# A two-layer decoder step on one Trainium2 core: where the feed-forward network applies the row scale, and how four small states are laid out and stored

## The chip, the cores and the metric

The program runs on one core of one Trainium2 chip. The core has a matrix engine, TensorE (PE in the profile; PEld is its weight load), and four others: VectorE (DVE), ScalarE (ACT), GpSimd (POOL) and SyncE (SP). Each takes its own instructions in order, and they meet through semaphores. Matrix products are accumulated in PSUM, in banks of 128 x 512 float32; everything else lies in SBUF, in 128 partitions. DMAs move data between the device memory and SBUF. In this program nearly all of them are issued by SP, one after the other; a few are issued by ACT.

The metric is the device time of one execution in microseconds (us); lower is better. Several executions are timed, and the median counts.

## The reference

One step of a hybrid decoder with 2 layers, for a prompt of 256 positions and 8 samples of one position each, so for T = 264 columns. Width is 1024, the inner width of the feed-forward network (FFN) is 2816. Each layer is a mixer with an input and an output projection, and then this FFN:

```python
def conv_ffn(x, prev, norm_g, w_gate, w_up, conv_w, conv_b, w_down):
    T = x.shape[1]
    h = rmsnorm(x, norm_g)
    g = h @ w_gate
    g_all = jnp.concatenate([prev, g], axis=1)
    gc = sum(conv_w[i] * g_all[:, i:i + T] for i in range(CONV_W)) + conv_b
    a = jax.nn.gelu(gc) * (h @ w_up)
    return x + a @ w_down, g_all[:, -(CONV_W - 1):]
```

`rmsnorm(x, g)` is `x * rsqrt(mean(x*x) + eps) * g`: a factor R for each position, and a gain for each feature. Since R belongs to the position, `(x * g) @ w * R` gives the same product as `rmsnorm(x, g) @ w`.

Layer 1 also has a pooling mixer (running means over windows of 2, 4, 8 and 16 positions). Outputs beside y are the keys and values of both layers, and states: the last 15 pooling inputs (`pool_prompt`, `pool_sample`) and the last 2 gate rows of the FFN (`ffn_conv_prompt`, `ffn_conv_sample`).

## The kernel before, in words

**Layout.** Activations are transposed: features on the 128 partitions, the 264 positions along the row. Every weight matrix is cut into blocks of 128 x 128, and the host packs all 1,472 blocks in the order in which PE uses them. To come near float32 accuracy, each operand is split into a high and a low part (`wh`, `wl` for weights, `..._h`, `..._l` for activations), and a block is three matmuls of 264 columns: high x high, high x low, low x high (`run`, L306).

**Weights.** SP loads chunks of 16 blocks (1 MB, tile `raw`, three buffers). `split` (L292) makes tiles of 8 blocks out of them: ACT copies the high part (L300) and DVE subtracts it for the low part (L301). There are four buffers of `wh` and of `wl`, and `split` runs three tiles ahead of PE.

**Phases.** For each layer: `in` (input projection, with attention and the other mixer woven in by hooks), `out` (output projection), `ff` (gate and up projection) and `dn` (down projection). In `ff` the order is gate 0, up 0, gate 1, up 1 and so on for 22 pairs; an output tile takes 8 blocks, 24 matmuls, and one of four PSUM banks (pool `psm`, `MMB = 4`). For the first four output tiles the blocks are taken in two halves.

**FFN.** `residual` (L589) leaves the operand `xg`: x times the gain, without R. The first `JN = 5` pairs multiply `xg`; R is multiplied in when the product leaves PSUM (L561 for the gate, L575 for up), and for up POOL then multiplies by the activated gate (L576). Meanwhile `normalise` (L549) builds a second operand `xn` that holds R: POOL multiplies x by R (L551), ACT makes the high part (L385) and DVE the low part (L386), for each of 8 tiles. Pairs 5 to 21 multiply `xn`; their gate is read from PSUM by the convolution itself (ACT L564, DVE L565 and L566, ACT L568), and one DVE instruction (L578) multiplies up by the activated gate. `halves` (L432) then splits the result `a` into its parts (ACT L433, DVE L434) for `dn`.

**States.** `CSTATE` holds the 2 old gate rows of the 8 samples for both layers, with the row index inside the feature index; `conv_prep` (L531) weights them on POOL and stores the newer row as `cs0` and `cs1` (L538). `PALL` has 16 places per feature group and sample: places 0 to 14 are loaded (L935), place 15 is written by `pool_in` (L1024), and places 1 to 15 are stored as `pools` (L1088). `plp`, the last 15 pooling inputs of the prompt, is stored as `poolp` (L1087).

**Order.** A scheduler of the framework orders each engine's instructions by its own estimate of time; instructions given to `keep_in_program_order` keep the order in which the code calls them. `late` (L274) is such a DMA on SP. Hooks (`blk(b, f)`) call f when b blocks of the phase have been issued. The stores of `k1`, `v1`, `poolp` and `pools` are plain DMAs: their place in SP's queue is the scheduler's. In the queue that results, `pools` and `poolp` stand behind the second `raw` load of layer 1's input projection and ahead of the loads of the cached values `V` (8 tiles in 16 DMAs).

**Layer 1's input projection.** Among its hooks: `pool_mix` (four products of the pooling mixer), `zs_score` and `zs_tr` (the samples' attention: scores, a scan `keep_s` and weights `zs` on ACT and DVE, and the transposes `pP` on PE), `z_qk` and `z_tr` (the prompt's attention).

Of the kernel before, what the change touches and what calls it, by code (L numbers as in the profile page):

```python
# [9 lines left out]
F32 = mybir.dt.float32  # L10
# [4 lines left out]
ALU = mybir.AluOpType  # L15
# [3 lines left out]
P = 128  # L19
D = 1024  # L20
KD = D // P
SEQ = 256
NS = 8
T = SEQ + NS
# [7 lines left out]
NF = DFF // P  # L32
# [1 line left out]


MMB = 4
JN = 5
KQ = 5
WARM = 12
YD = ((0, 1), (1, 3), (3, 5), (5, 7), (7, 8))  # L40

NA = 4
NB_ = 0.5
NEG = -1e30
SCALE = HD ** -0.5
POOLW = (2, 4, 8, 16)
NST = 15
# [106 lines left out]
def _consts():  # L154
# [35 lines left out]
_INS = [  # L190
    ("w", ((_NB - 16) * P * P,)), ("xw", (P * (KD + 16 * P + KD * T),)), ("x", (P, KD * T)), ("vec", (P, _NVEC)), ("cst", _CST_ARR.shape), ("rope", (P, 2 * T)),
    ("kt0", (NPHYS, P, 512)), ("vp0", (NPHYS, P, 512)), ("kt1", (NPHYS, P, 512)), ("vp1", (NPHYS, P, 512)),
    ("cstate", (P, 2 * NF * 2 * NS)), ("pstate", (P, 4 * NS * NST)),
    ("sguw", (P, 512)), ("sgub", (P, 512)), ("poolw", (P, 512)),
]
_OUTS = [
    ("y", (KD, P, T)), ("k0", (P, 4, T)), ("v0", (P, 4, T)), ("bvn", (P, 4, NS)),
    ("k1", (P, 4, T)), ("v1", (P, 4, T)), ("poolp", (P, 4, NST)), ("pools", (P, 4, NS, NST)),
    ("cv0", (P, NF, 10)), ("cv1", (P, NF, 10)), ("cs0", (P, NF, NS)), ("cs1", (P, NF, NS)),
]  # L200

# [2 lines left out]
def tile_decoder_step(ctx: ExitStack, tc: tile.TileContext, a):  # L204
    nc = tc.nc
    v, s, g = nc.vector, nc.scalar, nc.gpsimd
# [16 lines left out]
    con = ctx.enter_context(tc.tile_pool(name="con", bufs=1))  # L223
# [4 lines left out]
    sm = ctx.enter_context(tc.tile_pool(name="sm", bufs=3))  # L228
# [6 lines left out]
    def mv(name):  # L235
        return [f4(f"{name}_{x}", dt=F32R) for x in "hl"]

    def hl(tiles, k):
        return tiles[k // 4][0][:, k % 4, :], tiles[k // 4][1][:, k % 4, :]
# [4 lines left out]
    X = con.tile([P, KD, T], F32, name="X")  # L244
    VEC = con.tile([P, _NVEC], F32, name="VEC")
    CST = con.tile([P, _CST_ARR.shape[1]], F32, name="CST")
    PT = con.tile([1, NS * NPG], I32, name="PT")
    CSTATE = con.tile([P, 2, NF, 2, NS], F32, name="CSTATE")
    C0 = con.tile([P, 2, NF, NS], F32, name="C0")
    PALL = con.tile([P, 4, NS, 16], F32, name="PALL")  # L250

# [4 lines left out]
    def vec(n):  # L256
        o, w = _VEC[n]
        return VEC[:, o:o + w]
# [15 lines left out]
    def late(dst, src):  # L274
        tc.keep_in_program_order(nc.sync.dma_start(dst, src))
# [59 lines left out]
    orders = dict(_PHASES)  # L335
# [9 lines left out]
    first, o = [], 0  # L345
# [37 lines left out]
    def operand_tile(dst, m, src, gain, pin=False):  # L383
        h, l = dst[0][:, m % 4, :], dst[1][:, m % 4, :]
        i = s.activation(h, src, AF.Copy, scale=gain)  # L385
        j = v.scalar_tensor_tensor(l, src, gain, h.bitcast(F32), ALU.mult, ALU.subtract)  # L386
        if pin:
            tc.keep_in_program_order(i)
            tc.keep_in_program_order(j)
# [141 lines left out]
    def conv_prep(l):  # L531
        cw = vec("cw")
        w = lambda i: cw[:, (l * 3 + i) * NF:(l * 3 + i + 1) * NF].unsqueeze(2).to_broadcast([P, NF, NS])
        t = sm.tile([P, NF, NS], F32, tag="cprep", name=f"cprep{l}", bufs=1)
        g.tensor_tensor(C0[:, l], CSTATE[:, l, :, 0, :], w(0), ALU.mult)
        g.tensor_tensor(t, CSTATE[:, l, :, 1, :], w(1), ALU.mult)
        g.tensor_tensor(C0[:, l], C0[:, l], t, ALU.add)
        nc.sync.dma_start(a[f"cs{l}"], CSTATE[:, l, :, 1, :])  # L538

    def ffn(l, xg, R, down_evac, hooks=None):  # L540
        cw, cb = vec("cw"), vec("cb")
        wc = lambda i, j: cw[:, (l * 3 + i) * NF + j:(l * 3 + i) * NF + j + 1]
        cvo = sm.tile([P, NF, 10], F32, tag="cvo", name=f"cvo{l}", bufs=1)
        act = [mv(f"a{l}_{i}") for i in range((NF + 3) // 4)]
        xn = [mv(f"xn{l}{i}") for i in range(2)]
        gain = vec(f"f{l}")
        half = {}

        def normalise(m):  # L549
            z = sm.tile([P, T], F32, tag="rz", name=f"xr{l}{m}", bufs=4)  # L550
            g.tensor_tensor(z, X[:, m, :], R, ALU.mult)  # L551
            operand_tile(xn[m // 4], m, z, gain[:, m:m + 1])

        def evac(m, o):
            n, j = m
            if n == "g":
                wk = f4(f"wk{l}_{j}", (P, 2, T))
                C = wk[:, 0, :]
                if j < JN:
                    G = wk[:, 1, :]  # L560
                    v.tensor_tensor(G, o, R, ALU.mult)  # L561
                else:
                    G = o
                s.activation(C, G, AF.Identity, scale=wc(2, j), bias=cb[:, l * NF + j:l * NF + j + 1])  # L564
                v.scalar_tensor_tensor(C[:, 1:SEQ], G[:, 0:SEQ - 1], wc(1, j), C[:, 1:SEQ], ALU.mult, ALU.add)  # L565
                v.scalar_tensor_tensor(C[:, 2:SEQ], G[:, 0:SEQ - 2], wc(0, j), C[:, 2:SEQ], ALU.mult, ALU.add)  # L566
                v.tensor_tensor(C[:, SEQ:T], C[:, SEQ:T], C0[:, l, j, :], ALU.add)
                s.activation(cvo[:, j, :], G[:, SEQ - 2:T], AF.Copy)  # L568
                s.activation(C, C, AF.Gelu_apprx_tanh)
                half[j] = wk  # L570
            else:
                wk = half.pop(j)
                C, A = wk[:, 0, :], wk[:, 1, :]
                if j < JN:
                    v.tensor_tensor(A, o, R, ALU.mult)  # L575
                    g.tensor_tensor(A, A, C, ALU.mult)  # L576
                else:
                    v.tensor_tensor(A, o, C, ALU.mult)  # L578
                halves(*hl(act, j), A)

        hk = Hooks()
        for m in range(KD):
            hk.at(NA + NB_ * m, normalise, m)
        run(orders[f"ff{l}"], lambda m, k: hl(xg if m[1] < JN else xn, k), evac, hk)
        nc.sync.dma_start(a[f"cv{l}"], cvo)
        lnexp()
        run(orders[f"dn{l}"], lambda m, k: hl(act, k), down_evac, hooks)
# [22 lines left out]
    xg = [mv(f"xg_0{i}") for i in range(2)]  # L610
# [63 lines left out]
    q4, k4, v4 = f4("q4"), f4("k4"), f4("v4")  # L674
# [185 lines left out]
    hk = Hooks()  # L860
    fixed[0] = True
    blk = lambda b, f, *x: hk.at(b / 8 - 1, f, *x)
# [45 lines left out]
    hk = Hooks()  # L908
# [5 lines left out]
        blk(8, s_av, t)  # L914


    late(CSTATE, a["cstate"].rearrange("p (l j i s) -> p l j i s", l=2, j=NF, i=2))
    for l in range(2):
        conv_prep(l)

# [3 lines left out]
    R = nrm.finish()  # L924
# [7 lines left out]
    ffn(0, xg, R, evac, hk)  # L932


    late(PALL[:, :, :, 0:NST], a["pstate"].rearrange("p (g s i) -> p g s i", g=4, s=NS))  # L935
    xg = xg1
    q4, k4, v4 = f4("q4b"), f4("k4b"), f4("v4b")
    vt = f4("vt1", (P, 2, 512))
# [130 lines left out]
        blk(b, z_qk, t)  # L1069
    for t, b in enumerate((91, 104, 116)):  # L1070
        blk(b, z_tr, t)
    blk(100, lambda: nc.sync.dma_start(a["k1"], k4))
    for i, b in enumerate((62, 66, 70, 76)):
        blk(b, pool_mix, i)
    for t, b in enumerate((110, 118, 126)):
# [1 line left out]
    for i, b in enumerate((100, 108)):  # L1077
        blk(b, sample_av_of(st1, PZ, vtiles, i, "l1"))
    run(orders["in1"], pick(xg), in1_evac, hk)
    nc.sync.dma_start(a["v1"], v4)  # L1080
    hk = Hooks()
    blk(1, zs_out)
    blk(2, z_tr, 3)
    blk(6, lambda: v_pair(vt, v4[:, 3, :], 3, "v1"))
    for t in range(4):
        blk(9, z_av, t)
    nc.sync.dma_start(a["poolp"], plp)  # L1087
    nc.sync.dma_start(a["pools"], PALL[:, :, :, 1:16])  # L1088

    xg, nrm, evac = residual(vec("f1"), "f1")  # L1090
    run(orders["out1"], pick([catA, catB]), evac, hk)
# [12 lines left out]
def _lay(inp):  # L1104
    f = {n: np.asarray(x) for n, x in inp.items()}
    x = np.concatenate([f["x_prompt"].reshape(SEQ, D), f["x_sample"].reshape(NS, D)])
    col = lambda w: w.reshape(-1, P).T
    kt = lambda c: c[:, :, 0].reshape(NPHYS, P, 4, P).transpose(0, 3, 2, 1).reshape(NPHYS, P, 512)
    vecs = {"n1": col(f["l1_norm"]), "f0": col(f["ffn_norm"][0]), "f1": col(f["ffn_norm"][1]),
            "fin": col(f["final_norm"]), "sg": col(f["l0_sgu_gain"]), "ps": col(f["l1_pool_scale"]),  # L1110
            "cw": col(f["ffn_conv_w"].reshape(-1)), "cb": col(f["ffn_conv_b"].reshape(-1)),
            "w00": np.tile(f["l0_sgu_w"][:, 0, 0][None, :], (P, 1)), "b00": np.tile(f["l0_sgu_b"][:, 0][None, :], (P, 1))}
    ws = _pack_weights(f["l0_w_in"], f["l0_w_out"], f["l1_w_in"], f["l1_w_out"], f["ffn_w_gate"], f["ffn_w_up"], f["ffn_w_down"])
    xt = x.T.reshape(KD, P, T).transpose(1, 0, 2)
    return {
        "w": np.concatenate(ws[2:]),
        "xw": _pack_first(col(f["l0_norm"]), xt, ws),
        "x": xt.reshape(P, KD * T),
        "vec": np.concatenate([vecs[n] for n in _VEC], 1),
        "cst": _CST_ARR,  # L1120
        "rope": _ROPE,
        "kt0": kt(f["cache_l0_kv"]), "vp0": f["cache_l0_kv"][:, :, 1].reshape(NPHYS, P, 512),
        "kt1": kt(f["cache_l1_kv"]), "vp1": f["cache_l1_kv"][:, :, 1].reshape(NPHYS, P, 512),
        "pt": f["page_table"].reshape(1, NS * NPG),
        "cstate": f["state_ffn_conv"].reshape(2, NS, 2, NF, P).transpose(4, 0, 3, 2, 1).reshape(P, -1),
        "pstate": f["state_l1_pool"].reshape(NS, NST, 4, P).transpose(3, 2, 0, 1).reshape(P, -1),
        "sguw": f["l0_sgu_w"].transpose(2, 0, 1).reshape(P, 512),
        "sgub": np.tile(f["l0_sgu_b"].reshape(1, 512), (P, 1)),
        "poolw": f["l1_pool_w"].transpose(1, 0, 2).reshape(P, 512),
    }  # L1130
# [39 lines left out]
```

## Time and profile before

| | |
|---|---|
| time, median of 3 executions | 611.6 us (610.9 to 612.25) |
| the profiled execution | 612.44 us |
| its span, first to last instruction | 610.3 us |
| PE busy | 593.2 us, 97% of the span, 4908 matmuls |
| DVE busy | 417.4 us, 68% |
| ACT busy | 343.8 us, 56% |
| POOL busy | 66.7 us, 11% |
| bytes moved by DMA | 122.23 MB |

An execution is profiled by the hardware; 2.1 us of its time lie outside the span. The page lists groups of instructions as `line engine operation out<-in shape xcount | busy us, mean ns of one | idle us before, and what ended it`. The timeline lists `start us, duration us, engine line operation out<-in`, with the idle time of the engine before in brackets and what ended it. The chain of work is followed back from the last instruction, at each step to what released it. A busy matmul is longer than the distance to the next one, because they are pipelined; what counts is the distance from start to start. SPq and DVEq are the queues that issue.

### The profile page before, as it was taken

What the parts mean: (1) busy time and instruction counts of PE and PEld (TensorE: products, weight loads), DVE (VectorE), ACT (ScalarE), POOL (GpSimd) and SP (SyncE); (2) the same over time, 40 slices, a digit from 0 to 9 for tenths busy, and PEclk for the clock granted to TensorE, in tenths of its full rate; (3) what the DMA queues carried; (4) which work ended last, traced back from release to release, by engine and by line L of the source; (5) the groups of instructions that cost most, each with busy time, mean ns of one, the idle gap of its engine ahead of it and who ended that gap; (6) DMA issues with size and microseconds to landing.
All of it is one profiled execution on the core that took longest, in us unless ns stands there. A gap on an engine that the chain in (4) does not pass through costs nothing.

```text
span 610.3 us, 12279 instructions
## 1 busy us (share of the span) xinstructions
PE 593.2 (97%) x4908; PEld 573.3 (94%) x4908; DVE 417.4 (68%) x711; ACT 343.8 (56%) x607; POOL 66.7 (11%) x83
## 2 busy tenths in 40 slices
PE   8999999999999999999999799999999999999994
PEld 7988879999999999999999588999999999999994
DVE  6899566879776766655559276597986766754442
ACT  7757755576655555544454256566665555555441
POOL 4100002341000000011110000033300000001120
PEclk9999999999999999999999999999999999999998
DMA  8998936544654554894579992445365454564502
GB/s 324 347 396 293 333 123 173 200 147 139 213 202 164 182 205 150 333 333 166 201 178 86 262 356 106 169 154 198 133 214 177 169 207 158 189 209 154 199 1 71
DMA packets 41258, 122.23 MB, mean 200 GB/s; under 512 B 17138, under 2 KB 18546, under 8 KB 29810
## 3 DMA queue, kind: packets, MB, share of 16 engines
q1 hardware_dynamic: 40368, 120.25, 60.0%
q10 hardware_dynamic: 834, 1.20, 0.6%
q8 instruction: 38, 0.62, 0.4%
q14 instruction: 18, 0.15, 0.1%
HBM read 117.50 MB, written 3.94 MB: 199 GB/s over the span
## 4 chain that ended last, share of the span: by engine, by line
PE 71%; DVE 3%; DMA 2%; issue 1%; ACT 1%; POOL 0%; DVEq 0%; SPq 0%; ACTq 0%
PE mm L216 68%; DMA raw<-in_w 2%; DVE xn_l L386 1%; DVE wl L301 1%; PE pv_l L216 1%; PE Z L216 1%; PE pav L216 0%; DVE wk L565 0%; PE pt L219 0%; DVE X L1100 0%; DVE wk L566 0%; ACT wh L300 0%; POOL wk L576 0%; DVE wk L561 0%; PE vtp_v L219 0%
## 5 line engine op out<-in xcount | busy, mean ns | idle before, releaser
L301 DVE TENSOR_TENSOR wl<-raw,wh 128x1024 fp32r<-128x1024 f32 x179 | 220.4, 1231 | 132.7 <-ACT wh L300 130.8
L300 ACT ACTIVATE wh<-raw 128x1024 fp32r<-128x1024 f32 x179 | 189.6, 1060 | 184.4 <-PE mm L216 164.0
L216 PE MATMUL mm<-xn_h,wh 128*128 128x264 f32 x544 | 154.7, 284 | 0.0
L216 PE MATMUL mm<-xn_l,wh 128*128 128x264 f32 x544 | 154.5, 284 | 0.0
L216 PE MATMUL mm<-xn_h,wl 128*128 128x264 f32 x544 | 153.4, 282 | 0.0
L216 PEld LDWEIGHTS mm<-xn_h,wh 128*128 128x128 f32 x544 | 102.2, 188 | 0.2 <-ACT cvo L568 0.2
L216 PEld LDWEIGHTS mm<-xn_l,wh 128*128 128x128 f32 x544 | 102.2, 188 | 0.0
L216 PEld LDWEIGHTS mm<-xn_h,wl 128*128 128x128 f32 x544 | 102.2, 188 | 0.0
L216 PE MATMUL mm<-a_l,wh 128*128 128x264 f32 x352 | 99.8, 284 | 0.0
L216 PE MATMUL mm<-a_h,wh 128*128 128x264 f32 x352 | 99.7, 284 | 0.0
L216 PE MATMUL mm<-a_h,wl 128*128 128x264 f32 x352 | 99.3, 282 | 0.0
L216 PEld LDWEIGHTS mm<-a_l,wh 128*128 128x128 f32 x352 | 66.1, 188 | 0.0
L216 PEld LDWEIGHTS mm<-a_h,wl 128*128 128x128 f32 x352 | 66.1, 188 | 0.0
L216 PEld LDWEIGHTS mm<-a_h,wh 128*128 128x128 f32 x352 | 66.0, 188 | 0.0
L216 PE MATMUL mm<-xg_h,wh 128*128 128x264 f32 x160 | 48.2, 301 | 1.3 <-ACT xg_h L385 1.3
L216 PE MATMUL mm<-xg_f_h,wh 128*128 128x264 f32 x160 | 46.0, 288 | 2.0 <-DVE wk L575 2.0
L216 PE MATMUL mm<-xg_l,wh 128*128 128x264 f32 x160 | 46.2, 289 | 0.0
L216 PE MATMUL mm<-xg_h,wl 128*128 128x264 f32 x160 | 46.1, 288 | 0.0
L216 PE MATMUL mm<-xg_f_l,wh 128*128 128x264 f32 x160 | 45.4, 284 | 0.0
L216 PE MATMUL mm<-xg_f_h,wl 128*128 128x264 f32 x160 | 45.1, 282 | 0.0
L216 PE MATMUL mm<-xg_n_h,wh 128*128 128x264 f32 x128 | 39.2, 307 | 0.0
L216 PE MATMUL mm<-xg_n_l,wh 128*128 128x264 f32 x128 | 36.9, 288 | 0.0
(249 smaller groups left out, 1055.5 us busy)
## 6 DMA issues: line engine op xcount, KB each, us to landing
raw<-in_w SPq DMA_DIRECT2D x89, 1024.0 KB, 4.9
K<-in_kt SPq DMA_DIRECT2D x32, 256.0 KB, 6.1
V<-in_vp SPq DMA_DIRECT2D x32, 256.0 KB, 7.2
raw<-in_w SPq DMA_DIRECT2D x4, 512.0 KB, 5.8
X<-in_x SPq DMA_DIRECT2D x4, 264.0 KB
xw<-in_xw SPq DMA_DIRECT2D x2, 388.0 KB, 5.6
out_k<-k SPq DMA_DIRECT2D x1, 528.0 KB
out_v<-v SPq DMA_DIRECT2D x1, 528.0 KB
```

Source lines behind the costliest of these rows:

```text
L216: return self.keep(nc.tensor.matmul(*x, **k))
L300: s.activation(h, src, AF.Copy)
L301: v.tensor_tensor(l, src, h.bitcast(F32), ALU.subtract)
L386: j = v.scalar_tensor_tensor(l, src, gain, h.bitcast(F32), ALU.mult, ALU.subtract)
```

## The change

In the FFN the operand `xn`, `normalise` and its hooks go. All 22 pairs multiply `xg`, and each product is multiplied by R on DVE as it leaves PSUM. The convolution always reads that SBUF copy, and up is always multiplied by the activated gate on POOL. `CSTATE` is laid out with the row index outside, so that a partition's part of `cs0` or `cs1` is one run of 176 floats. `PALL` is loaded and stored whole, 16 places instead of 15 (the host pads the input and drops one place of the output). `poolp`, `pools`, `k1` and `v1` go through `late`, at fixed block numbers.

```diff
-JN = 5
-NA = 4
-NB_ = 0.5
...
-    CSTATE = con.tile([P, 2, NF, 2, NS], F32, name="CSTATE")
+    CSTATE = con.tile([P, 2, 2, NF, NS], F32, name="CSTATE")
...
-        g.tensor_tensor(C0[:, l], CSTATE[:, l, :, 0, :], w(0), ALU.mult)
-        g.tensor_tensor(t, CSTATE[:, l, :, 1, :], w(1), ALU.mult)
+        g.tensor_tensor(C0[:, l], CSTATE[:, l, 0], w(0), ALU.mult)
+        g.tensor_tensor(t, CSTATE[:, l, 1], w(1), ALU.mult)
         g.tensor_tensor(C0[:, l], C0[:, l], t, ALU.add)
-        nc.sync.dma_start(a[f"cs{l}"], CSTATE[:, l, :, 1, :])
+        nc.sync.dma_start(a[f"cs{l}"], CSTATE[:, l, 1])
...
-        xn = [mv(f"xn{l}{i}") for i in range(2)]
-        gain = vec(f"f{l}")
         half = {}
-
-        def normalise(m):
-            z = sm.tile([P, T], F32, tag="rz", name=f"xr{l}{m}", bufs=4)
-            g.tensor_tensor(z, X[:, m, :], R, ALU.mult)
-            operand_tile(xn[m // 4], m, z, gain[:, m:m + 1])
 
         def evac(m, o):
             n, j = m
             if n == "g":
                 wk = f4(f"wk{l}_{j}", (P, 2, T))
                 C = wk[:, 0, :]
-                if j < JN:
-                    G = wk[:, 1, :]
-                    v.tensor_tensor(G, o, R, ALU.mult)
-                else:
-                    G = o
+                G = wk[:, 1, :]
+                v.tensor_tensor(G, o, R, ALU.mult)
...
-                if j < JN:
-                    v.tensor_tensor(A, o, R, ALU.mult)
-                    g.tensor_tensor(A, A, C, ALU.mult)
-                else:
-                    v.tensor_tensor(A, o, C, ALU.mult)
+                v.tensor_tensor(A, o, R, ALU.mult)
+                g.tensor_tensor(A, A, C, ALU.mult)
                 halves(*hl(act, j), A)
 
-        hk = Hooks()
-        for m in range(KD):
-            hk.at(NA + NB_ * m, normalise, m)
-        run(orders[f"ff{l}"], lambda m, k: hl(xg if m[1] < JN else xn, k), evac, hk)
+        run(orders[f"ff{l}"], pick(xg), evac)
...
-    late(PALL[:, :, :, 0:NST], a["pstate"].rearrange("p (g s i) -> p g s i", g=4, s=NS))
+    late(PALL, a["pstate"].rearrange("p (g s i) -> p g s i", g=4, s=NS))
...
-    blk(100, lambda: nc.sync.dma_start(a["k1"], k4))
+    blk(84, late, a["poolp"], plp)
+    blk(84, late, a["pools"], PALL)
+    blk(112, late, a["k1"], k4)
...
-    nc.sync.dma_start(a["v1"], v4)
     hk = Hooks()
...
-    nc.sync.dma_start(a["poolp"], plp)
-    nc.sync.dma_start(a["pools"], PALL[:, :, :, 1:16])
+    blk(12, late, a["v1"], v4)
```

More of the change, by code (lines that the diff above doesn't have):

```diff
@@ L192 @@
     ("kt0", (NPHYS, P, 512)), ("vp0", (NPHYS, P, 512)), ("kt1", (NPHYS, P, 512)), ("vp1", (NPHYS, P, 512)),
-    ("cstate", (P, 2 * NF * 2 * NS)), ("pstate", (P, 4 * NS * NST)),
+    ("cstate", (P, 2 * NF * 2 * NS)), ("pstate", (P, 4 * NS * 16)),
     ("sguw", (P, 512)), ("sgub", (P, 512)), ("poolw", (P, 512)),
@@ L197 @@
     ("y", (KD, P, T)), ("k0", (P, 4, T)), ("v0", (P, 4, T)), ("bvn", (P, 4, NS)),
-    ("k1", (P, 4, T)), ("v1", (P, 4, T)), ("poolp", (P, 4, NST)), ("pools", (P, 4, NS, NST)),
+    ("k1", (P, 4, T)), ("v1", (P, 4, T)), ("poolp", (P, 4, NST)), ("pools", (P, 4, NS, 16)),
     ("cv0", (P, NF, 10)), ("cv1", (P, NF, 10)), ("cs0", (P, NF, NS)), ("cs1", (P, NF, NS)),
@@ L914, in tile_decoder_step @@
         blk(8, s_av, t)
-    late(CSTATE, a["cstate"].rearrange("p (l j i s) -> p l j i s", l=2, j=NF, i=2))
+    late(CSTATE, a["cstate"].rearrange("p (l i j s) -> p l i j s", l=2, i=2, j=NF))
     for l in range(2):
@@ L1124, in _lay @@
         "pt": f["page_table"].reshape(1, NS * NPG),
-        "cstate": f["state_ffn_conv"].reshape(2, NS, 2, NF, P).transpose(4, 0, 3, 2, 1).reshape(P, -1),
-        "pstate": f["state_l1_pool"].reshape(NS, NST, 4, P).transpose(3, 2, 0, 1).reshape(P, -1),
+        "cstate": f["state_ffn_conv"].reshape(2, NS, 2, NF, P).transpose(4, 0, 2, 3, 1).reshape(P, -1),
+        "pstate": np.pad(f["state_l1_pool"].reshape(NS, NST, 4, P).transpose(3, 2, 0, 1), ((0, 0), (0, 0), (0, 0), (0, 1))).reshape(P, -1),
         "sguw": f["l0_sgu_w"].transpose(2, 0, 1).reshape(P, 512),
@@ L1160 @@
     poolp = o["poolp"].transpose(2, 1, 0).reshape(1, NST, 512)
-    pools = o["pools"].transpose(2, 3, 1, 0).reshape(NS, NST, 512)
+    pools = o["pools"][..., 1:].transpose(2, 3, 1, 0).reshape(NS, NST, 512)
     cvp, cvs = [], []
```

## The prediction

> **What bounds the kernel now.** I read the page first (shares of the span, then the groups), then a table of windows, the waits summed by pair, the chain that ended last, and the timelines of PE, DVE, POOL and SP where PE stops.
>
> ```profile
> span 610.3 us, 12279 instructions
> PE 593.2 (97%) x4908; PEld 573.3 (94%) x4908; DVE 417.4 (68%) x711; ACT 343.8 (56%) x607; POOL 66.7 (11%) x83
> ...
> 200.00:260.00 60.00, 60.00 (x498) 60.00 (x497) 40.09 (x65) 33.37 (x59) 0.00 (x0) 1.00 0.60 214
> 324.00:340.00 16.00, 16.00 (x152) 14.72 (x155) 12.94 (x31) 5.71 (x7) 0.00 (x0) 1.00 1.48 37
> ...
> PE pP L219 <- DVE zs L965: 3.9, 1, 3.9
> PE mm L216 <- DVE wk L575: 2.0, 2, 1.0
> ```
>
> The windows' columns are: length, then PE, PEld, DVE, ACT and POOL busy with counts, granted clock, DMA share, GB/s. In a quiet stretch one matmul leaves every 60.00/498 = 0.1205 us; an output tile of the FFN (24 matmuls) takes 2.89 us, a pair 5.78. PE is the bound, so this change, which leaves the number of products alone, can only win or lose where PE stops. Two lines name those places, and the timeline of PE shows what each costs:
>
> ```profile
> 139.34 0.28 PE L216 MATMUL mm<-xg_f_h,wl 128*128 128x264 f32 x1
> 140.63 0.36 PE L216 MATMUL mm<-xg_f_h,wh 128*128 128x264 f32 x1 [1.01 <-DVE wk L575]
> ...
> 346.53 0.28 PE L216 MATMUL mm<-xg_n_h,wl 128*128 128x264 f32 x1
> 350.70 0.69 PE L219 MATMUL pP<-CST,zs 128*128 128x128 f32 x2 [3.89 <-DVE zs L965]
> 351.04 0.57 PE L216 MATMUL mm<-xg_n_h,wh 128*128 128x264 f32 x1
> 353.82 0.29 PE L216 MATMUL mm<-xg_n_h,wh 128*128 128x264 f32 x1
> ...
> 432.59 0.36 PE L216 MATMUL mm<-xg_f_h,wh 128*128 128x264 f32 x1 [1.02 <-DVE wk L575]
> ```
>
> From start to start, each FFN stop costs 140.63 - 139.34 - 0.12 = 1.17 us; the one at 432.59 has the same idle time, so the same price: 2.3 us together. The stop in layer 1's input projection costs 350.70 - 346.53 - 0.12 = 4.05, and PE comes out of it slow: the 12 steps from 351.04 to 353.82 take 2.78 us instead of 1.45, so 1.33 more, and 0.1 for the two transposes: 5.5 us. Everything removable that I find is 7.8 us, 1.3%.
>
> **The change, part by part.**
>
> *1. The second operand goes.* Why PE stops in the FFN stands in DVE's queue (chain of work, which joins neighbours of one group):
>
> ```profile
> 131.69 0.66 DVE wk L561 x2
> 132.37 1.22 DVE wl L301
> 133.58 2.62 DVE xn_l L386 x4
> 136.21 0.90 DVE wk L565
> 140.15 0.35 DVE wk L575
> ```
>
> The bank that PE wants at 139.5 holds the product of up 1, which L575 takes out at 140.15. It stands behind the four low parts of `xn` (2.62 us). Without them, L575 moves to about 140.15 - 2.62 = 137.5, some 2 us before PE asks. The instruction order of the changed kernel moves it further: there L575 stands ahead of the second weight split, behind one `wl` (to 133.6) and a convolution, so I put the bank free at 135 to 136. So the stop goes in both layers: -2.3. Late next would be the split of weights, which runs three tiles (3 x 2.89 us) ahead.
>
> Also removed are, per layer, 8 copies on ACT and these, for both layers and for layer 0:
>
> ```profile
> L551 POOL TENSOR_TENSOR xr<-X,R_f 128x264 f32<-128x264 f32 x16 | 13.0, 844 | 14.0 <-ACT R_f L423 7.5 <-DVE xn_l L386 3.3 <-issue 3.3
> L386 DVE SCALAR_TENSOR_TENSOR xn_l<-xr,VEC,xn_h 128x264 fp32r<-128x264 f32 x8 | 4.9, 676 | 0.0
> ```
>
> That is 6.5 us of POOL and 4.9 or more of DVE per layer. They lie beside PE, so their time beyond that stop is worth nothing.
>
> *2. R at the eviction of all pairs.* Added per layer: 17 gate multiplies on DVE (0.42 us, below) and 17 POOL multiplies; up costs DVE the same single instruction as before. The first five pairs already run this form, and one cycle of it is in the trace:
>
> ```profile
> 152.30 0.42 DVE L575 TENSOR_TENSOR wk<-mm,R_f 128x264 f32<-128x264 f32 x1
> 152.64 1.22 DVE L301 TENSOR_TENSOR wl<-raw,wh 128x1024 fp32r<-128x1024 f32 x1
> 152.95 1.52 POOL L576 TENSOR_TENSOR wk<-wk 128x264 f32<-128x264 f32 x1 [2.46 <-ACT wk L569]
> 154.50 0.42 ACT L433 ACTIVATE a_h<-wk 128x264 fp32r<-128x264 f32 x1 [1.94 <-POOL wk L576]
> 154.84 1.04 ACT L300 ACTIVATE wh<-raw 128x1024 fp32r<-128x1024 f32 x1
> 155.91 1.23 DVE L301 TENSOR_TENSOR wl<-raw,wh 128x1024 fp32r<-128x1024 f32 x1 [0.52 <-ACT wh L300]
> 157.97 1.22 DVE L301 TENSOR_TENSOR wl<-raw,wh 128x1024 fp32r<-128x1024 f32 x1
> 140.66 0.75 POOL L576 TENSOR_TENSOR wk<-wk 128x264 f32<-128x264 f32 x1 [2.93 <-DVE wk L575]
> L576 POOL TENSOR_TENSOR wk<-wk x10: 754/1216/1863, 129.4 to 444.5; 128x264 f32<-128x264 f32 x10
> ```
>
> In the last line the numbers are shortest, median and longest in ns. This is the new wait: ACT's in-order queue stands at `a_h` until POOL is done, and the next `wh`, hence the next `wl` and DVE's evictions behind it, stand behind `a_h`. The cycle is L575 at 152.30, POOL to 154.47, `a_h`, `wh`, `wl`, convolution, next L575 at about 157.97 (where the row shows the following `wl` start): 5.67 us. PE needs 5.78 for a pair. It closes, just. POOL's multiply is in it with 1.52 us; the longest of ten, 1.86, makes 6.01, the shortest, 0.75, 4.90. The median (1.22) makes 5.37, so over 22 pairs nothing accumulates. A single long turn is covered: four banks let DVE fall behind by three tiles, 8.7 us, less about 1 us for an eviction and the wait around it. By DVE's load there is room: from 200 to 260 it was busy 40.09 of 60 us, 3.86 per pair, and gets one gate multiply more, 4.3 of 5.78. I take 0. Ends: 0, and the cost of a cycle longer than PE's, below among the rivals. For a gain there is no room, as PE has no idle time in these pairs.
>
> POOL's 1.52 is the number to weigh: it ran while `wl` (152.64 to 153.86) ran and ended 0.61 us after it, and alone it takes 0.75. [...]
>
> *3. States and stores.* The other stop, by SP's timeline, a DVE and an ACT row, and the chain:
>
> ```profile
> 322.37 0.58 SPq L1088 DMA_DIRECT2D out_pools<-PALL  x1
> 323.01 7.76 SPq L1087 DMA_DIRECT2D out_poolp<-plp  x1
> 330.97 2.61 SPq L275 DMA_DIRECT2D V<-in_vp  x2
> 333.64 0.42 SPq L275 DMA_DIRECT2D raw<-in_w  x1
> ...
> 323.84 1.21 DVE L301 TENSOR_TENSOR wl<-raw,wh 128x1024 fp32r<-128x1024 f32 x1
> 347.20 1.06 ACT L300 ACTIVATE wh<-raw 128x1024 fp32r<-128x1024 f32 x1 [9.73 <-DMA raw<-in_w]
> ...
> 333.64 13.46 DMA raw<-in_w
> 347.20 1.07 ACT wh L300
> 350.22 0.44 DVE zs L965
> ```
>
> `pools` writes 128 x 4 x 8 = 4096 pieces of 60 bytes. Behind it SP is held 7.76 us in issuing `poolp`, then 2.61 in two `V` loads, so a weight load whose buffer was free at 323.84 + 1.21 = 325.05 is issued at 333.64, 8.6 us late. It lands after 13.46 us, in a stretch in which the DMA engines were busy with few bytes (37 GB/s), and ACT stands before it 9.73 us. `zs` and PE come 3.50 us behind `wh`.
>
> In the changed kernel this load stands behind one `V` tile and ahead of the stores, so it can issue at about 325.1. Bounds for its flight: the group's usual 4.9 us (the page's median for these loads, below) and 13.46 again.
>
> ```profile
> raw<-in_w SPq DMA_DIRECT2D x89, 1024.0 KB, 4.9
> DMA packets 41258, 122.23 MB, mean 200 GB/s; under 512 B 17138, under 2 KB 18546, under 8 KB 29810
> ```
>
> So it lands between 330.0 and 338.6. PE does not wait if it lands by 346.53 + 0.12 - 3.50 = 343.1. Both ends lie 4 us or more before that: -5.5, slow restart included. I take a value near the short end, as the stores come later and are now runs of 512 bytes a feature group. Late next: the transposes of the prompt's last attention tiles, with a margin I put at 0.5 to 0.8 us, and `zs`, about 3 us; I take 0 for both, with an upper end of 3 us as a rival.
>
> Moved on SP: `poolp` and `pools` to behind the tenth or eleventh `V` load, `k1` and `v1` to later blocks. Their issue can hold SP for up to the 7.76 us seen; SP is then ahead by the `V` loads and the next `raw`, so the price is 0 to a stop of the same kind, half or less of 5.5. The states `cs0`, `cs1` and the load of `PALL` lose 2 x 128 x 22 = 5632 and 4096 small pieces. The waits show no PE stop at either; worth 0. With `pools`, 13,824 of 17,138 packets under 512 bytes go.
>
> **Sum.** 612.44 - 2.3 (part 1) + 0 (part 2) - 5.5 (part 3) = 604.6 for the profiled execution. That execution is 0.84 above the median of 611.6, so by the median 603.8.
>
> **The rivals.**
>
> *The FFN's cycle outgrows PE (slower).* Place: `a_h` and `wh` on ACT, from pair 5 on, in both layers. If every POOL multiply waits for a second `wl` or delays one (1.14 us, its start-to-start step), the cycle is 5.67 + 1.14 = 6.81, 1.03 more than PE's pair. After 22 pairs, less 7.7 us of slack, 15 us per layer: 603.8 + 30 = 634. It takes the time past 612.8 once the cycle is above 6.33 us in all pairs ((9.0/2 + 7.7)/22 = 0.55 over 5.78). [...] Against it: five pairs per layer ran so with the `xn` work on top, and the longest multiply gives 6.01. Chance 0.10.
>
> *The FFN stop stays.* Something else ahead of L575 (the two 1.22 us `wl`, or slower POOL work) keeps the bank: 603.8 + 2.3 = 606.1. Against it: the 2.62 us that go are over twice the stop. Chance 0.11.
>
> *The stores bite elsewhere.* Issued later, in the crowd of `V` loads, they hold back the next `raw` or `V`, and PE stops for the prompt's or samples' attention: 3 to 5.5 us come back, 607 to 609. For it: 7.76 us in one issue. Chance 0.08.
>
> *No change.* The late load came from the `V` and `K` traffic rather than from the stores, and the FFN stop returns too: 611 to 612. Chance 0.03.
>
> **How the numbers follow.** The forecast has 0.68, with a range of its own of 603.0 to 605.3. Adding the kept FFN stop and most of the third case, up to 608.4, and a little below for neighbours of the stops that also shorten, gives 602.8 to 608.4 with some 0.85; outside lie the slower case, no change and the tail. What can be told from no change here is 0.2%, 1.2 us: faster holds 0.68 + 0.11 + 0.08 = 0.87, same 0.03, slower 0.10.
>
> **What the changed profile would show.** Right: the waits no longer list PE behind L575 for 2.0 nor behind `zs` for 3.9; PE's share rises to 98%; the `raw` load at 325 is issued within 2 us of its buffer; packets under 512 bytes fall to about 3,300; POOL's L576 has 44 with a median near 1.2 us; a window inside layer 0's FFN has PE busy throughout. Wrong: PE waits with DVE L561 or L575 named, spread over the late pairs (the first rival); a long wait at `pP`, `pt` or `pv` near 330 to 360 (the third); L576 with a median over 1.9 us.

## The result and the profile after

The changed kernel takes 603.91 us (median of 4 runs, 602.43 to 604.2), the kernel before 611.92 (610.9 to 613.54): a ratio of 0.9862, with a 95% interval of 0.9834 to 0.9889. The profiled execution takes 603.97 us. Ratios, and the time given for `after_again`, leave out four executions: three of 830 us, with a granted clock of about 0.66, and one of 2053 us. The page of the profiled execution:

```profile
span 602.1 us, 12388 instructions
PE 590.7 (98%) x4908; PEld 571.7 (95%) x4908; DVE 420.4 (70%) x729; ACT 340.4 (57%) x591; POOL 109.5 (18%) x101
...
DMA packets 27948, 122.28 MB, mean 203 GB/s; under 512 B 3314, under 2 KB 4978, under 8 KB 16498
```

The same 4908 matmuls, 2.5 us less of PE's busy time, 8.2 us less of span. PE's own list of waits has five entries now; four of them lie in the first 41 us and one at the end (`ns_fin`):

```profile
PE warm L213 <- DVE warm L368: 1.2, 1, 1.2
PE S L213 <- DVE k L673: 1.2, 1, 1.2
PE mm L213 <- ACT xg_h L382: 0.9, 1, 0.9
PE ns_fin L213 <- ACT sq_fin L395: 0.6, 1, 0.6
PE mm L213 <- DVE wl L610: 0.3, 1, 0.3
```

The waits for the FFN's eviction (2.0 us) and for `zs` (3.9 us) are gone. Where the time went is best read from four matmuls that every kernel here has, the sums of squares in front of each norm. First PE's timeline before, then after (each line is two matmuls):

```profile
120.85 0.61 PE L216 MATMUL ns_f<-acc_f,ones 128*128 128x264 f32 x2
313.93 0.61 PE L216 MATMUL ns_n<-acc_n,ones 128*128 128x264 f32 x2
412.80 0.61 PE L216 MATMUL ns_f<-acc_f,ones 128*128 128x264 f32 x2
601.25 0.61 PE L216 MATMUL ns_fin<-acc_fin,ones 128*128 128x264 f32 x2
```

```profile
120.96 0.61 PE L213 MATMUL ns_f<-acc_f,ones 128*128 128x264 f32 x2
312.51 0.60 PE L213 MATMUL ns_n<-acc_n,ones 128*128 128x264 f32 x2
405.84 0.61 PE L213 MATMUL ns_f<-acc_f,ones 128*128 128x264 f32 x2
593.04 0.61 PE L213 MATMUL ns_fin<-acc_fin,ones 128*128 128x264 f32 x2
```

They cut the run into a start (to 120.85), layer 0's FFN, layer 1's mixer and layer 1's FFN. The differences of the starts give what each stretch gained: +0.11, then (312.51 - 120.96) - (313.93 - 120.85) = -1.53, -5.54 and -1.25, in all -8.21. The same was done for each experiment. The medians come from several executions; the stretches come from one profiled execution each, as changes against the profiled execution of before, in us:

| kernel | median | start | FFN 0 | mixer 1 | FFN 1 |
|---|---|---|---|---|---|
| changed | 603.91 | +0.11 | -1.53 | -5.54 | -1.25 |
| e1_ffn_only | 608.06 | -1.26 | -1.53 | -1.18 | -1.25 |
| e2_states_only | 607.89 | +1.01 | -0.01 | -5.48 | 0.00 |
| e3_whole_only | 606.76 | -0.07 | -0.02 | -5.53 | 0.00 |
| e4_order_only | 613.03 | -0.11 | -0.01 | +0.76 | -0.01 |
| e5_pool_twice | 604.40 | +0.15 | -1.15 | -5.52 | -0.88 |
| e6_up_on_dve | 604.94 | +0.88 | -1.16 | -5.52 | -0.87 |
| e7_xn_kept | 606.39 | +0.28 | -0.18 | -5.54 | +0.08 |
| e8_xn_later | 609.09 | +1.48 | -1.52 | -1.74 | -1.25 |
| after_again | 604.33 | +0.48 | -1.53 | -5.54 | -1.25 |
| e9_twice_held | 631.61 | -1.04 | +12.33 | -5.48 | +12.57 |
| e10_plain_place | 603.10 | -0.08 | -1.52 | -5.48 | -1.25 |
| e11_scores_later | 603.16 | -0.55 | -1.53 | -5.53 | -1.25 |

Two columns of this table warn against reading an effect from the total. The start varies by more than 2 us among kernels whose instructions there are the same (PE's wait of `S` for `k` was 1.2 us in the changed kernel, 2.2 in e2 and not there in e1). And the stop for `zs`, where it is left, has no fixed size (e1 and e8 have it too). The FFN columns repeat to 0.02 among kernels with the same FFN.

On SP and in the stretch of the former stop the changed kernel shows this: the timeline of SP, the DMA issues of the load issued at 323.66 (its last number is the time to landing), and the windows:

```profile
323.66 0.34 SPq L272 DMA_DIRECT2D raw<-in_w  x1
...
339.43 1.25 SPq L272 DMA_DIRECT2D out_poolp<-plp  x1
340.74 0.66 SPq L272 DMA_DIRECT2D out_pools<-PALL  x1
...
raw<-in_w SPq DMA_DIRECT2D x1, 1024.0 KB, 4.8
...
324.00:340.00 16.00, 16.00 (x162) 14.04 (x161) 12.76 (x30) 6.05 (x9) 0.00 (x0) 1.00 0.76 271
```

The load that took 13.46 us takes 4.8, and the DMA engines move 271 GB/s at a share of 0.76, where they moved 37 at 1.48.

### The profile page after: what moved, and what is told of

It is laid out like the page before. It is cut to its first block, busy times and chain, and to the rows that moved or that the text cites. A ratio compares the mean times of both kernels' runs of the same rounds, so it can differ in the third digit from the quotient of the medians.

```text
span 602.1 us, 12388 instructions
## 1 busy us (share of the span) xinstructions
PE 590.7 (98%) x4908; PEld 571.7 (95%) x4908; DVE 420.4 (70%) x729; ACT 340.4 (57%) x591; POOL 109.5 (18%) x101
## 4 chain that ended last, share of the span: by engine, by line
PE 92%; DVE 3%; DMA 2%; SPq 1%; issue 1%; ACT 0%; ACTq 0%; DVEq 0%
PE mm L213 84%; DMA raw<-in_w 1%; PE pv_l L213 1%; PE sc L213 1%; DVE wl L298 1%; PE pav L213 1%; PE pt L216 1%; DMA PT<-in_pt 1%; PE Z L213 1%; PE S L213 1%; SPq L338 1%; PE pf L213 0%; DVE X L1081 0%; DVE rz_q L667 0%; PE pm L213 0%
## 5 line engine op out<-in xcount | busy, mean ns | idle before, releaser
L213 PE MATMUL mm<-xg_f_h,wh 128*128 128x264 f32 x704 | 200.5, 285 | 0.0
L213 PE MATMUL mm<-xg_f_l,wh 128*128 128x264 f32 x704 | 199.9, 284 | 0.0
L213 PE MATMUL mm<-xg_f_h,wl 128*128 128x264 f32 x704 | 198.6, 282 | 0.0
L213 PEld LDWEIGHTS mm<-xg_f_l,wh 128*128 128x128 f32 x704 | 132.2, 188 | 0.1
L213 PEld LDWEIGHTS mm<-xg_f_h,wh 128*128 128x128 f32 x704 | 132.2, 188 | 0.1
L213 PEld LDWEIGHTS mm<-xg_f_h,wl 128*128 128x128 f32 x704 | 132.2, 188 | 0.0
L562 POOL TENSOR_TENSOR wk<-wk 128x264 f32<-128x264 f32 x44 | 67.6, 1538 | 194.4 <-DVE wk L561 150.4
L430 ACT ACTIVATE a_h<-wk 128x264 fp32r<-128x264 f32 x44 | 18.7, 425 | 76.1 <-POOL wk L562 76.1
L431 DVE TENSOR_TENSOR a_l<-wk,a_h 128x264 fp32r<-128x264 f32 x44 | 19.2, 437 | 44.4 <-ACT a_h L430 44.4
```

What stands on the lines that cost most here:

```text
L213: return self.keep(nc.tensor.matmul(*x, **k))
L430: s.activation(h, src, AF.Copy)
L431: v.tensor_tensor(l, src, h.bitcast(F32), ALU.subtract)
```

## The experiments

**The two parts alone.** e1 is before with the FFN part of the diff, e2 is before with all of the rest.

> The FFN part alone; states and stores as before. My theory (the four low parts of xn ahead of L575 on DVE make the FFN stop; the stores make the other): PE's two waits for the eviction go, the wait for zs stays with 3.9 us and its slow restart; 2.3 us below before, 609.3 to 609.7. Rival (the two parts are tied, or the FFN stop has another cause): the FFN waits stay and the time is within 1 us of before.

> The states and stores alone; FFN as before. My theory: the wait for zs goes, 5.5 us below before, 606.1 to 606.7; PE still waits twice 1.0 us for the eviction. Rival (a new late transfer takes its place): 607 to 609 with a wait of PE between 330 and 380 us.

e1: 608.06 us (606.87 to 608.91), ratio to before on that chip 0.9938 (0.9921 to 0.9955); e2: 607.89 (606.88 to 609.75), 0.9935 (0.9912 to 0.9957). In the stretches the two parts separate: e1 gets -1.53 and -1.25 in the FFNs, e2 gets -5.48 in the mixer and nothing in the FFNs. Each total missed its expectation by more than 1 us, and the table says why: e1 had no wait of `S` in its start and a shorter stop for `zs` (2.6 us idle), e2 had a start that was 1.0 us longer. The starts vary like that among kernels that are the same there. The shorter stop of e1 stays open: e8, which also lacks the FFN stop, has a shorter one too (2.8 us), so that the two parts may not be wholly independent there.

**Pieces or order.** The change to the stores is two in one: whole rows, and another place in SP's queue. e3 takes the rows alone, for `pools` and `PALL`, e4 the places alone.

```diff
 e3, against before (host side likewise)
-    late(PALL[:, :, :, 0:NST], a["pstate"]...)
+    late(PALL, a["pstate"]...)
...
-    nc.sync.dma_start(a["pools"], PALL[:, :, :, 1:16])
+    nc.sync.dma_start(a["pools"], PALL)

 e4, against before
+    blk(84, late, a["poolp"], plp)
+    blk(84, late, a["pools"], PALL[:, :, :, 1:16])
+    blk(112, late, a["k1"], k4)
-    blk(100, lambda: nc.sync.dma_start(a["k1"], k4))
...
-    nc.sync.dma_start(a["v1"], v4)
...
-    nc.sync.dma_start(a["poolp"], plp)
-    nc.sync.dma_start(a["pools"], PALL[:, :, :, 1:16])
+    blk(12, late, a["v1"], v4)
```

> Before, with PALL loaded and stored in one piece per row; the store keeps its place in SP's queue, ahead of V and of the weight load. Theory of pieces (4096 runs of 60 bytes hold SP and the DMA engines): poolp's issue falls from 7.8 us to about 1, the weight load is issued at about 325 and lands by 339, the stop goes: 606 to 607. Theory of order (what stands ahead of the load matters, not its pieces): the load is still issued after 330, the stop stays at least by half, 609 to 612. I hold the first to be likelier, 0.7.

> Before, with the four stores issued at the fixed block numbers of the changed kernel, but pools still in 4096 runs of 60 bytes. Theory of order: the late weight load goes ahead of the stores, the stop is gone, 606.1 to 606.7. Theory of pieces: the small pieces, now issued at about 341, hold up the weight load that follows them (issued at 345.6 in the changed kernel) by about 8 us or the last V loads; PE stops somewhere between 345 and 375 for 1 to 4 us, 607 to 611.

e3: 606.76 us (605.58 to 606.99), ratio 0.9907 (0.989 to 0.9923). e4: 613.03, ratio 1.001 (0.9992 to 1.0029). SP's timeline of e3, and the landing time of its `pools`:

```profile
322.28 0.34 SPq L1088 DMA_DIRECT2D out_pools<-PALL  x1
322.68 0.42 SPq L1087 DMA_DIRECT2D out_poolp<-plp  x1
323.30 1.69 SPq L275 DMA_DIRECT2D V<-in_vp  x2
325.04 0.42 SPq L275 DMA_DIRECT2D raw<-in_w  x1
...
out_pools<-PALL SPq DMA_DIRECT2D x1, 256.0 KB, 3.9
```

The stores stand where they stood, ahead of the load; `poolp` takes 0.42 us to issue instead of 7.76, the load goes out at 325.04 and the whole 5.5 us are won. The new layout of `CSTATE` is not in e3, and e2, which has it, gains no more in any stretch behind the start; it has no experiment of its own. In e4 the store kept its small pieces:

```profile
341.15 0.59 SPq L275 DMA_DIRECT2D out_pools<-PALL  x1
341.99 15.39 SPq L275 DMA_DIRECT2D V<-in_vp  x2
...
out_pools<-PALL SPq DMA_DIRECT2D x1, 240.0 KB, 19.8
...
PE pv_l L216 <- DMA V<-in_vp: 3.6, 1, 3.6
```

It takes 19.8 us to land, SP is held 15.39 us in the next two loads, and the stop is back in another place: PE waits for the last `V` tile. The mixer stretch is 0.76 us longer than before. So the pieces made the stop, and the order only chose who waited. e10 is the counter-check: the changed kernel with the stores at their old places.

```diff
 e10, against the changed kernel
-    blk(84, late, a["poolp"], plp)
-    blk(84, late, a["pools"], PALL)
-    blk(112, late, a["k1"], k4)
...
+    nc.sync.dma_start(a["poolp"], plp)
+    nc.sync.dma_start(a["pools"], PALL)
...
```

> The changed kernel with the four stores at the places that the scheduler gives them (pools and poolp ahead of V and of the weight load, k1 and v1 as before). My theory now (pieces alone made the late load): the same as the changed kernel within 1 us, no wait for zs. Rival (with whole rows the order still counts): 1 us or more slower, with PE waiting between 340 and 380 us.

603.10 us (602.53 to 603.85), ratio 0.9857 (0.9822 to 0.9893), the same as the changed kernel in every stretch after the start, to 0.06 us. SP issues `pools` at 320.77 there and the load behind it at 323.48. With whole rows the place is worth nothing. On the same chip the changed kernel was run again as a measure.

> The changed kernel once more, on the chip of the next three, as their measure: 603 to 605.

It took 603.3, 604.33 and 607.58 us.

**What stopped the FFN.** e7 is the changed kernel that still computes the second operand, with `normalise` at its old hooks, and does not use it; e8 is before with that work 10 tiles later.

```diff
 e7, against the changed kernel (NA = 4, NB_ = 0.5 and normalise as in before)
...
+        for m in range(KD):
+            hk.at(NA + NB_ * m, normalise, m)
-        run(orders[f"ff{l}"], pick(xg), evac)
+        run(orders[f"ff{l}"], pick(xg), evac, hk)

 e8, against before
-JN = 5
+JN = 11
-NA = 4
+NA = 14
```

> The changed kernel with normalise kept at its old place and its operand unused. My theory (the low parts of xn on DVE make the FFN stop): the two waits for L575's successor come back with 1.0 to 1.2 us each, 2.3 us above the changed kernel, 606 to 606.7. Rival (the stop came from the scheduler's place for L575 or from the change of the operand): no wait, 603 to 605.

> Before, with normalise started 10 tiles later and 11 pairs instead of 5 on the operand without R. My theory: the burst costs PE only where DVE is already behind, at the first pairs; later it is paid from the slack of 8.7 us: both stops go, 2.3 us below before, 609 to 610. Rival (the burst of 2.6 us of DVE makes a stop wherever it stands): the stop moves to the later place with 1 us or more a layer, 611 to 612.5.

e7: 606.39 us, ratio to before 0.9931 (0.9912 to 0.9949). Its waits, and two entries of DVE's timeline, the low parts of `xn` and the eviction that PE waits for:

```profile
PE mm L215 <- DVE wk L570: 2.0, 2, 1.0
...
133.78 2.71 DVE L385 SCALAR_TENSOR_TENSOR xn_l<-xr,VEC,xn_h 128x264 fp32r<-128x264 f32 x4
140.35 0.42 DVE L570 TENSOR_TENSOR wk<-mm,R_f 128x264 f32<-128x264 f32 x1
```

Both stops are back with their old size, with every pair on `xg` and R multiplied in at all of them: it is the work on the second operand, at that place, that makes them. In the changed kernel DVE takes the same product out at 135.34. e7 does not separate the 2.71 us of the low parts from two things that came back with them: the scheduler puts convolutions and a `wl` between them and that eviction, and POOL runs its four multiplies for `xn` meanwhile. e8: 609.09 us, ratio 0.9962 (0.9942 to 0.9981). The FFN stretches are those of the changed kernel to 0.01 us, although eight low parts per layer are still computed and used; no wait for an eviction of the FFN is left. So the second operand was not too dear, it stood in the wrong place. The rest of e8's profiled time is its start and a stop for `zs`.

**The cycle through POOL.** e5 puts a second, unused multiply ahead of each of POOL's (its result goes nowhere), e6 moves POOL's multiply to DVE.

```diff
 e5, against the changed kernel
...
                 v.tensor_tensor(A, o, R, ALU.mult)
+                g.tensor_tensor(dum, A, C, ALU.mult)
                 g.tensor_tensor(A, A, C, ALU.mult)

 e6, against the changed kernel
-                g.tensor_tensor(A, A, C, ALU.mult)
+                v.tensor_tensor(A, A, C, ALU.mult)
```

> The changed kernel with a second, unused POOL multiply ahead of each of the 44. My theory (DVE, POOL and ACT form a cycle of 5.89 us a pair, PE's pair is 5.81, and the four banks hide the difference): the cycle grows by 0.75 (a multiply alone) to 6.64; 0.83 a pair over 18 pairs is 15 us a layer, less some 5.7 us of slack still free: 9 us a layer, 622 us, with PE waiting for L561 or L550 in the late pairs. Rival (POOL is not in a cycle, ACT and DVE go round it): 603 to 605.

> The changed kernel with the 44 multiplies on DVE in place of POOL. My theory: the cycle shortens to 4.4 to 5.2 us, the evictions no longer fall behind, but PE did not wait, so 603 to 605. [...] Other rival (DVE becomes the bound): slower than 605 with PE waiting in the FFN.

e5: 604.40 us (603.52 to 606.28), ratio 0.9895 (0.9867 to 0.9923), a plain miss of the expected 622. e6: 604.94 (604.54 to 605.41), 0.9898 (0.988 to 0.9916), as expected: no gain, and 0.37 us more in each FFN, the same as in e5. In both, PE stops once a layer for the eviction of a gate (0.2 us idle and slow steps around it, near 134 and 420 us). ACT's timeline shows why e5 missed, first the changed kernel, then e5:

```profile
202.63 0.42 ACT L430 ACTIVATE a_h<-wk 128x264 fp32r<-128x264 f32 x1 [1.82 <-POOL wk L562]
202.96 1.04 ACT L297 ACTIVATE wh<-raw 128x1024 fp32r<-128x1024 f32 x1
```

```profile
204.03 1.07 ACT L297 ACTIVATE wh<-raw 128x1024 fp32r<-128x1024 f32 x1 [0.61 <-PE mm L213]
205.38 0.43 ACT L430 ACTIVATE a_h<-wk 128x264 fp32r<-128x264 f32 x1 [0.29 <-POOL wk L564]
```

With the longer POOL work the scheduler put the next `wh` ahead of `a_h`, which opens the cycle. The experiment had changed two things. e9 repeats it with ACT and DVE held to the order that they have in the changed kernel, from pair 5 on:

```diff
 e9, against e5 (keep pins an instruction behind the last one traced on its engine;
 low parts of weights and the gelu are emitted one step later, to fit that order)
-                v.tensor_tensor(A, o, R, ALU.mult)
+                keep(v.tensor_tensor(A, o, R, ALU.mult))
+                flush("wl")
                 g.tensor_tensor(dum, A, C, ALU.mult)
                 g.tensor_tensor(A, A, C, ALU.mult)
...
+                keep(s.activation(h, A, AF.Copy))
+                keep(v.tensor_tensor(lo, A, h.bitcast(F32), ALU.subtract))
```

> The second, unused POOL multiply again, but ACT and DVE are held to the order that they have in the changed kernel, from pair 5 on (the scheduler had moved a_h behind the next wh). My theory of the cycle, as it stands now: 5.89 plus 0.75 to 0.83 (a multiply alone) is 6.6 to 6.7 us a pair, 0.85 above PE's 5.81; over 17 pairs 14 us, less 5.6 us of slack (8.7 less 1 for an eviction less 2.1 already used): 8 to 9 us a layer, 620 to 623, PE waiting for L551 or L562. Rival (the order does not close a cycle): 603 to 606.

631.61 us (630.5 to 632.09), ratio 1.0329 (1.0292 to 1.0366). Two evictions of up by DVE, one product, and PE's wait:

```profile
200.64 0.43 DVE L579 TENSOR_TENSOR wk<-mm,R_f 128x264 f32<-128x264 f32 x1
207.37 0.43 DVE L579 TENSOR_TENSOR wk<-mm,R_f 128x264 f32<-128x264 f32 x1
...
206.38 0.39 PE L213 MATMUL mm<-xg_f_h,wl 128*128 128x264 f32 x1 [0.65 <-DVE wl L306]
...
PE mm L213 <- DVE wl L306: 18.3, 28, 0.7
```

The cycle is 6.73 us, just above what was expected (6.6 to 6.7), and PE is tied to it. The 0.84 us that it is longer than the changed kernel's lie wholly in POOL's part: `a_h` starts 3.05 us behind the eviction (at 203.69) where it took 2.21 (202.63 - 200.42), and from there to the next eviction it is 3.68 us in both. But PE does not wait for an eviction, as expected, it waits for a weight's low part. By stretches it costs 13.9 and 13.8 us a layer against the changed kernel, where 8 to 9 were expected: the slack is the lead of the weights, and the held order had used up most of that where it set in (the lead of a tile over its first product fell from 4.4 to 1.1 us there). The held order without the second multiply was not run, so how much of the 13.9 us that loss of lead explains is not shown.

**One step further.** The largest wait that is left in the changed kernel is that of `S` for `k` near 40 us. e11 issues these products five blocks later.

```diff
-    for t, b in enumerate((82, 95, 108, 121)):
+    for t, b in enumerate((87, 95, 108, 121)):
```

> The changed kernel with the first attention scores of layer 0 five blocks later (87 in place of 82). PE waits there 1.1 to 2.2 us for k on DVE; five blocks are 1.8 us of other products. If nothing behind it gets late: 0.8 to 1.5 us below the changed kernel. Rival (the softmax or the transposes of these tiles come late instead): no change or slower.

603.16 us (602.75 to 603.32), ratio to before 0.9859 (0.9824 to 0.9894). The wait went, and a new one of 0.5 us (`pmu` for `bsum`) came behind it; the start is 0.5 to 1.0 us shorter than in the other runs of that chip that had the wait. Against e10's 603.10 and the spread of the changed kernel, that is not a gain that these runs can tell. None of the kernels tried beats the changed one clearly.

## Why the prediction was right, and where it was not

The forecast of 603.8 us met 603.91. That it did so to 0.1 us is luck, as the starts alone vary by more than 2 us. Both stops went, and by the size that was stated; three steps of the working were wrong all the same: the length of the FFN's cycle, what covers it, and why the load was late.

**Part 1, the FFN stop: right, -2.3 forecast, -2.78 measured** (1.53 + 1.25). e7 and e8 show that the work on the second operand, by its place, is the cause. The bank was forecast free at 135 to 136, and DVE's eviction there runs from 135.34 to 135.76. The 0.5 us not counted are a slow step behind each stop (0.20 us instead of 0.12) and, in layer 0, two slow steps at 158.31 (0.28 and 0.23 us). There the weight load waited 0.2 us for `cvo` (L568 at 158.08), the last read of the first gate that the convolution takes from PSUM itself. e7 no longer has this wait, and its layer 0 is 0.18 us shorter than before's.

**Part 2, R at the eviction: 0 forecast, 0 measured, by two errors.** DVE, POOL and the lead of the weights in the changed kernel's layer 0:

```profile
200.42 0.43 DVE L561 TENSOR_TENSOR wk<-mm,R_f 128x264 f32<-128x264 f32 x1
200.77 1.21 DVE L298 TENSOR_TENSOR wl<-raw,wh 128x1024 fp32r<-128x1024 f32 x1
201.03 1.57 POOL L562 TENSOR_TENSOR wk<-wk 128x264 f32<-128x264 f32 x1 [4.32 <-DVE wk L561]
203.09 0.43 DVE L431 TENSOR_TENSOR a_l<-wk,a_h 128x264 fp32r<-128x264 f32 x1 [1.10 <-ACT a_h L430]
204.04 1.23 DVE L298 TENSOR_TENSOR wl<-raw,wh 128x1024 fp32r<-128x1024 f32 x1 [0.17 <-ACT wh L297]
206.31 0.43 DVE L561 TENSOR_TENSOR wk<-mm,R_f 128x264 f32<-128x264 f32 x1
...
L562 POOL TENSOR_TENSOR wk<-wk x44: 752/1578/1618, 129.5 to 533.4; 128x264 f32<-128x264 f32 x44
...
153.62 1.22 DVE L298 TENSOR_TENSOR wl<-raw,wh 128x1024 fp32r<-128x1024 f32 x1
236.13 1.22 DVE L298 TENSOR_TENSOR wl<-raw,wh 128x1024 fp32r<-128x1024 f32 x1
...
160.16 0.28 PE L213 MATMUL mm<-xg_f_h,wl 128*128 128x264 f32 x1
241.55 0.28 PE L213 MATMUL mm<-xg_f_h,wl 128*128 128x264 f32 x1
```

The cycle is 206.31 - 200.42 = 5.89 us, not 5.67. The step that failed is "next L575 at about 157.97": I let it follow the convolution at once, 0.83 us behind the end of the `wl` (157.14); it comes 1.04 us behind it (206.31 - 205.27). POOL's multiply has a median of 1.58 us, not about 1.2, as 42 of the 44 now start beside a `wl`. PE's pair is (241.55 - 160.16) / 14 = 5.81 by the last two rows, 14 pairs apart, and not 5.78: the 498 matmuls of that window include some that only reach into it. So "over 22 pairs nothing accumulates" was wrong: 0.08 us a pair does. The cover was misnamed too: not four banks with 8.7 us, but the lead of the weight tiles (in e9 PE waits for `wl`), 6.6 us where nothing holds the split back. The low part made at 153.62 is done at 154.84 and first multiplied at 160.16, a lead of 5.3 us; that made at 236.13, 14 pairs later, has a lead of 241.55 - 237.35 = 4.2 us. The last two tiles of layer 1's FFN have 3.6 and 3.9. The change is free because this lead outlasts 22 pairs; at 0.08 us a pair, 3.6 us would cover some 45 more (an estimate). In e6, without POOL in the cycle, the evictions keep PE's 5.81 and the lead stays at 6.5.

POOL's multiply at 201.03 takes 1.57 us beside a `wl` and ends 0.62 us after it; one without a `wl` beside it, at 137.48, takes 0.75. The row at 140.66 in the prediction, 0.75 too, is not one alone: a `wl` starts at 140.75 and takes 1.74 us, where the median is 1.23. What makes them longer beside each other the rows do not show. The multiplies are twice as long beside a `wl`, and that still costs nothing here: e6, which has them on DVE, is no faster.

**Part 3, the stores: the size right (-5.5 forecast, -5.54 measured), the cause half wrong.** I credited the load's place "ahead of the stores" and took the runs of 512 bytes as a bonus. e3, e4 and e10 show the reverse: the whole rows (2 KB a partition, not runs of 512 bytes) are worth all of it, the place nothing. The flight was at the short end of its bounds, 4.8 us. By the size of the pieces: 240 KB in runs of 60 bytes landed in 19.8 us in e4, 256 KB in whole rows in 3.9 in e3 and 6.4 in the changed kernel. Packets under 512 bytes were forecast at about 3,300 and are 3314.

**The rivals.** *The FFN's cycle outgrows PE* was priced at 15 us a layer and 634 us, for a cycle of 6.81; e9 has 6.73, 13.9 a layer and 631.6. That PE pays for such a cycle, e9 shows; its premise, that every multiply waits for a second `wl` or delays one, no run shows: in the changed kernel the longest of the 44 takes 1.62 us, and the `wl` beside them take 1.21 to 1.23. That its price came close is partly luck, as it took 22 pairs and 7.7 us of slack in the banks, where PE waited in 14 pairs a layer (28 waits) and the lead of the weights had 1.1 us left. It also left out that the scheduler can go round the cycle (e5). *The stores bite elsewhere* is what e4 shows, for a change of order without the change of layout; there all 5.5 us come back, and 0.8 more. *The FFN stop stays* did not come: with the second operand gone, e1 and the changed kernel have no such wait. *No change* is refuted by the stretches.

**The sum.** 604.6 was forecast for the profiled execution, which took 603.97: 0.5 us more came from the FFN, and the rest lies in the start and outside the span; the start alone varies by more than that.

## What to carry to other kernels

Where a transfer arrives late, look at what was issued ahead of it and how small its pieces are, before moving anything: one store in 60-byte runs cost 3.8 to 5.5 us at its old place (e8, e1, before) and 6.3 at another (e4), against the kernels with whole rows. A cycle of engines that comes out just under the bound's own time is not safe because it closes; compare it with what covers a miss (here the weights' lead of 6.6 us against 0.08 us a pair) and count how many rounds there are. And an experiment that lengthens one instruction under a scheduler tests the scheduler too; hold the order, or read it first.

## What the runs showed of the hardware

PE's slow restart did not depend on the length of the stop alone. PE's timeline of e1, then of e8, where the stop for `zs` ends:

```profile
346.58 0.66 PE L216 MATMUL pP<-CST,zs 128*128 128x128 f32 x2 [2.56 <-DVE zs L946]
...
347.26 0.42 PE L213 MATMUL mm<-xg_n_l,wh 128*128 128x264 f32 x1
347.48 0.42 PE L213 MATMUL mm<-xg_n_h,wl 128*128 128x264 f32 x1
```

```profile
349.59 0.44 PE L219 MATMUL pP<-CST,zs 128*128 128x128 f32 x2 [2.83 <-DVE zs L965]
...
349.99 0.28 PE L216 MATMUL mm<-xg_n_l,wh 128*128 128x264 f32 x1
350.11 0.28 PE L216 MATMUL mm<-xg_n_h,wl 128*128 128x264 f32 x1
```

After 2.56 us of idle time e1's steps are 0.22 us, for 12 of them, and the granted clock is 0.50 from 347 to 350 us; after 2.83 us e8's steps are 0.12 from 349.99 on, and the granted clock stays at 1.00. In before, after 3.89 us, the steps are 0.22 as well, with a granted clock of 0.50 from 351 to 353 us. What decides the restart, the runs do not show.

Beside POOL's multiply an instruction of DVE was longer as well. In e5, DVE and POOL:

```profile
204.65 0.72 DVE L555 TENSOR_TENSOR wk<-wk,C 128x8 f32<-128x8 f32 x1
...
204.53 0.82 POOL L564 TENSOR_TENSOR wk<-wk 128x264 f32<-128x264 f32 x1
```

DVE's addition of 8 columns, 0.16 us elsewhere in that stretch, takes 0.72 and ends with POOL's multiply, at 205.37 and 205.35.
